# A hybrid DeltaNet and attention trunk on one core: input squares on two engines, first weights behind x, and three small reorderings

## Chip, cores and metric

The kernel runs on one core of one Trainium2 chip. The core has five engines with a queue each: TensorE (PE in the profile) multiplies matrices into PSUM, VectorE (DVE) and ScalarE (ACT) do elementwise work, GpSimd (POOL) sets constants, and SyncE (SP) issues most of the DMAs. Each engine works its queue in order and waits at an instruction until what it needs is there. The metric is the device time of one execution in microseconds (us), lower is better. Given are three runs and one profiled execution.

## The reference

A trunk of two layers over 512 tokens with 1024 channels, in float32. Every mixer and every MLP reads an RMS-normalised copy of the residual stream h and adds its result to h.

```python
def rmsnorm(x, w):
    y = x * lax.rsqrt(jnp.mean(x * x, axis=-1, keepdims=True) + EPS)
    return y * w
...
h = x
# layer 0: gated DeltaNet, then a gated MLP with a causal conv of width 3
h = h + gated_deltanet(rmsnorm(h, a_norm_w), a_w_in, ...)
h = h + conv_gated_mlp(rmsnorm(h, ffn_norm_w[0]), ...)
# layer 1: K and V projected once from h; sliding-window attention, then the MLP
k, v = shared_kv(h, kv_norm_w, w_kv)
h = h + sliding_window_sink_attention(rmsnorm(h, b_norm_w), k, v, b_w_q, ..., b_w_o)
h = h + conv_gated_mlp(rmsnorm(h, ffn_norm_w[1]), ...)
return rmsnorm(h, final_norm_w)
```

Three places of it matter here. The first is the very first norm, with the start of the DeltaNet's input projection (its keys first, then 16 gate pairs per token: a sigmoid, and an exponential of `a_log` times a softplus). The second is the attention's output projection, `o @ w_o`, over 1024 channels of the heads. The third is the end of the last MLP with the final norm.

## The kernel before

**Layout and precision.** The residual stream is held with channels on the 128 partitions and the 512 tokens along the row: eight tiles `hT[0..7]` of 128 x 512. A float32 product is made of three products in a reduced format: each factor is split into a high part and a rest, and `mm3` (L158) sums high x high (L162), high x rest (L163) and rest x high (L164) for each of the eight blocks of 128 channels. A weight block is loaded by SP into a buffer called `stage` (128 x 8 x 256, two buffers), and `cast` (L128) makes the high part `whi` on ScalarE (L132) and the rest `wlo` on VectorE (L133). There are three buffers for each of them.

**What sets the order.** The program is written once, straight through. A planner lays every instruction into its engine's queue: it goes by a priority, which is the program order unless the source says otherwise, and by what it expects to be ready. The source moves priorities for the DeltaNet stage (`ORDER`, L30), fixes TensorE's order by hand in attention (L1357), and can pin one instruction behind another on the same engine with `behind(later, earlier)` (L176), which orders the issue and adds no other wait. Waits on data, on freed buffers and on DMAs are put in by the planner.

**Input stage (L201 to L335).** SP loads the four x tiles of 128 tokens x 1024 channels (L204) and then the first stage of the input projection, the key weights, as two halves of 128 columns (L210). The identity for transposes is made on GpSimd, and five rows of norm weights are loaded on ScalarE's queue and turned into columns, `normc` (L232 to L237). For each x tile `xs[c]`, ScalarE squares it and sums along the row (L258), and takes the root of the mean (L259); VectorE takes the reciprocal (L260) and scales the tile (L261). TensorE then turns each block of 128 channels for all four tiles (L266), and `split_scaled` (L171) makes the high part `xh` on ScalarE (L172) and the rest `xl` on VectorE (L173). Then comes the first key projection, with the conv (L277, L280) and a Silu (L281). The second `stage` buffer is next used for the gates' weights, `gst`: GpSimd clears 48 columns of each block (L307), ScalarE's queue loads two groups of 16 columns (L309, L310), it is cast and multiplied with 48 columns. `nega` takes an Exp of `a_log` (L319); ScalarE's roots and its Exp need different function tables, and a change of table is an instruction of its own in the profile (ACT_TABLE_LOAD). Some further rows, the gates' constants among them, are loaded on SP (L232, L316, L317, L736).

**Output projection of attention (L1320 to L1386).** The eight output tiles need all 16 heads. The first three tiles are opened early, in three PSUM banks `d`, and are filled for the heads that are ready (`early_outputs`, `late_outputs`). The last block of heads comes at L1378 to L1382: nine products, pass by pass (high x high for the three tiles, then rest x high, then high x rest), and an add into `hT[m]` on VectorE after the last of each tile. The loop from L1383 on casts weights for tiles 3 to 7 and multiplies.

**The end (L1100 to L1159).** `final` squares the first seven tiles of the result on ScalarE, sums the squares on VectorE in `acc`, and weights the tiles with the final norm's weights. The last tile's down projection is done in two halves of 256 tokens, each in two parts (`last_down`). When a half is complete, VectorE adds it to `h7` (L1150), and `finish` squares it on ScalarE (L1131), weights it (L1132) and adds the squares to `acc` (L1133) on VectorE; TensorE turns the last four blocks of each of the two token tiles (L1118) and sums `acc` over the channels with a product with a column of ones, one for each token tile (L1137); then come root (L1138) and reciprocal (L1139). Two scaled copies per token tile, one on VectorE (L1146) and one on ScalarE (L1144), go out by SP (L1147). `finish(0)` stands between the two parts of the second half.

Of the kernel before, what the change touches and what calls it, by code (L numbers as in the profile page):

```python
# [17 lines left out]
P = 128  # L18
T = 512
NC = T // P  # L20
D = 1024
# [3 lines left out]
HQK = 8  # L25
# [16 lines left out]
def kernel(  # L42
# [27 lines left out]
    V, S, G, PE, SP = nc.vector, nc.scalar, nc.gpsimd, nc.tensor, nc.sync  # L70
# [130 lines left out]
    xs = []  # L201
# [3 lines left out]
        xs.append(xt)  # L205
    win = a_w_in[0]
    first = wpool.tile([P, 8, 256], F32, tag="stage", bufs=2, name=nm("stage"))
    for i in range(2):
        cs = slice(HQK * P + i * P, HQK * P + (i + 1) * P)
        SP.dma_start(first[:, :, i * P : (i + 1) * P], win[:, cs].rearrange("(k p) c -> p k c", p=P))  # L210
# [44 lines left out]
    for c in range(NC):  # L255
        junk = main.tile([P, D], F32, tag="nt", bufs=2, name=nm("junk"))
        r = const([P, 1], s="rx")
        S.activation(junk[:], xs[c], AF.Square, accum_out=r[:])  # L258
        S.activation(r[:], r[:], AF.Sqrt, bias=epsc[:, 0:1], scale=1.0 / D)  # L259
        V.reciprocal(r[:], r[:])  # L260
        V.tensor_scalar(xs[c][:], xs[c][:], r[:, 0:1], None, op0=ALU.mult)  # L261
    xh, xl = [], []
# [56 lines left out]
    S.activation(nega[32:48, :], gp16[32:48, 0:1], AF.Exp)  # L319
# [780 lines left out]
    def final(h, last_down):  # L1100
        hw, acc = [], None
        for k in range(KD):
            t = r2("xh")
            hw.append(t)
            if k == KD - 1:
                break
            V.tensor_scalar(t[:], h[k], onw_c[:, 9 + k : 10 + k], None, op0=ALU.mult)
            sq = r2("sum" if acc is None else "hsq")
            S.activation(sq[:], h[k], AF.Square)
            if acc is None:  # L1110
                acc = sq
            else:
                V.tensor_tensor(acc[:], acc[:], sq[:], op=ALU.add)

        def turned(hf, c, tag):
            pt = bank(tag)
            for k in range(4):
                PE.transpose(pt[:, k * P : (k + 1) * P], hw[4 * hf + k][:, c * P : (c + 1) * P], ident[:])  # L1118
            return pt

        halves = [bank("d") for _ in range(2)]
        S.activation(warm[:], acc[:, 0:1], AF.Sqrt)
        front = [turned(0, c, t) for c, t in enumerate(["s", "s", "p", "g"])]
        h7, w7 = h[KD - 1], hw[KD - 1]
        sq7 = r2("hsq")
        rt = const([P, NC], s="rt")
        ts = [slice(0, 256), slice(256, 512)]

        def finish(u):
            cs = slice(2 * u, 2 * u + 2)  # L1130
            S.activation(sq7[:, ts[u]], h7[:, ts[u]], AF.Square)  # L1131
            V.tensor_scalar(w7[:, ts[u]], h7[:, ts[u]], onw_c[:, 16:17], None, op0=ALU.mult)  # L1132
            V.tensor_tensor(acc[:, ts[u]], acc[:, ts[u]], sq7[:, ts[u]], op=ALU.add)  # L1133
            back = [turned(1, 2 * u, "d"), turned(1, 2 * u + 1, "s" if u else "d")]
            ps = bank("g")
            for c in (2 * u, 2 * u + 1):
                PE.matmul(ps[:, c : c + 1], acc[:, c * P : (c + 1) * P], onec, start=True, stop=True)  # L1137
            S.activation(rt[:, cs], ps[:, cs], AF.Sqrt, bias=epsc[:, 0:1], scale=1.0 / D)  # L1138
            V.reciprocal(rt[:, cs], rt[:, cs])  # L1139
            for c in (2 * u, 2 * u + 1):  # L1140
                for hf, pt in enumerate((front[c], back[c % 2])):
                    y = r2("xl")
                    if hf:
                        S.activation(y[:], pt[:], AF.Copy, scale=rt[:, c : c + 1])  # L1144
                    else:
                        V.tensor_scalar(y[:], pt[:], rt[:, c : c + 1], None, op0=ALU.mult)  # L1146
                    SP.dma_start(out[0, c * P : (c + 1) * P, hf * T : (hf + 1) * T], y[:])  # L1147

        def add(u):
            V.tensor_tensor(h7[:, ts[u]], h7[:, ts[u]], halves[u][:, 0:256], op=ALU.add)  # L1150
# [12 lines left out]

    def attention(h):
# [192 lines left out]
        with tc.manual_schedule(engines={mybir.EngineType.PE}):  # L1357
            stream = dense()
            for u in range(16):
                scores(u)  # L1360
                if u > 1:
                    values(u - 2)
                if u == 1:
                    take(stream, 8)
                if u > 0:
                    turn_back(u - 1)
                take(stream, 4 if u == 1 else 12 if u < 12 else 11)
            for _ in stream:
                pass
            rest = late_outputs(opened, range(begun, KD - 1))  # L1370
            take(rest, 9)
            turn_back(15)
            values(14)
            take(rest, 5)
            values(15)
            for _ in rest:
                pass
            for i in range(3):  # L1378
                for m, (ps, w) in enumerate(opened):
                    PE.matmul(ps[:], w[i % 2][:, KD - 1, :], (ah, ah, al)[i][-1], start=False, stop=i == 2)  # L1380
# [64 lines left out]
```

## Time and profile before

| what | value |
|---|---|
| median of 3 runs (lowest, highest) | 1416.39 us (1415.27, 1416.59) |
| profiled execution, its own time | 1418.66 us |
| span of the profiled execution | 1416.8 us |
| mean granted TensorE clock | 0.998 |
| busy TensorE, VectorE, ScalarE, GpSimd | 98%, 78%, 53%, 1% |
| first product of the input projection | 13.63 us |
| longest wait of TensorE after that, up to 46 us | 1.72 us |
| start of the last scaled output copy on VectorE | 1411.56 us |
| last output DMA issued | 1413.0 us |

A line of the order of time reads: start, length, engine and source line, operation, output <- inputs by the program's names, shapes, count, and in brackets how long the engine was idle before it and what ended the wait. "SPq" and "ACTq" are DMA issues in a queue, "PEld" is TensorE loading weights, which overlaps its products. Products are pipelined: a product of 512 columns is shown with about 0.39 us, but the next one starts 0.23 us after it. Each of the sums of L1137 is shown as two records.

### The profile page before, as it was taken

The numbers are of one execution on the slowest core, as the hardware profiler recorded it, in microseconds if no ns is written. First come the engines' busy times: TensorE is split into PE (matmuls) and PEld (weight loads), VectorE is DVE, ScalarE is ACT, GpSimd is POOL, SyncE is SP. The second block draws the span as 40 slices with busy tenths as digits, with TensorE's granted clock in tenths as the row PEclk, the third lists the DMA queues.
The fourth block names the chain that finished last, engine by engine and source line by source line (L and its number), as shares of the span: only waits on it lengthen the run. The fifth ranks groups of instructions, "written<-read, shape, count | busy, mean of one in ns | idle before, by whom it ended". The sixth has DMA issues, their size and how long they took to land.

```text
span 1416.8 us, 21740 instructions
## 1 busy us (share of the span) xinstructions
PE 1384.8 (98%) x8362; PEld 1166.5 (82%) x8362; DVE 1109.1 (78%) x2072; ACT 748.0 (53%) x1470; POOL 15.7 (1%) x37
## 2 busy tenths in 40 slices
PE   7999999999999999999999999999999999999997
PEld 5787888878877888888988889778788888988897
DVE  4996886968856447879878889788658888878996
ACT  7764576656647325444335446567544444444543
POOL 1000000000100000000000000000000000000000
PEclk9999999999999999999999999999999999999999
DMA  5333254172465323221443223322132221432222
GB/s 160 90 104 115 80 174 124 60 230 84 143 221 157 119 86 115 90 90 46 134 149 119 75 73 108 109 76 76 60 112 86 93 90 59 137 107 86 95 75 75
DMA packets 162299, 151.80 MB, mean 107 GB/s; under 512 B 24148, under 2 KB 150677, under 8 KB 162197
## 3 DMA queue, kind: packets, MB, share of 16 engines
q1 hardware_dynamic: 159938, 150.22, 33.0%
q8 instruction: 66, 1.08, 0.3%
q10 hardware_dynamic: 2259, 0.20, 0.1%
q14 instruction: 36, 0.29, 0.1%
HBM read 133.60 MB, written 15.75 MB: 105 GB/s over the span
## 4 chain that ended last, share of the span: by engine, by line
PE 85%; DVE 7%; DMA 4%; ACT 2%; issue 1%; SPq 0%; DVEq 0%; ACTq 0%
PE d L162 20%; PE d L164 20%; PE d L163 20%; PE g L198 2%; DVE wlo L133 2%; PE d L1207 1%; PE d L1211 1%; PE d L1209 1%; PE d L1054 1%; PE d L1052 1%; PE d L1053 1%; PE s L1054 1%; PE p L1303 1%; PE s L659 1%; PE s L1052 1%
## 5 line engine op out<-in xcount | busy, mean ns | idle before, releaser
L162 PE MATMUL d<-xh,whi 128*128 128x512 f32 x1128 | 444.2, 394 | 0.2
L163 PE MATMUL d<-xl,whi 128*128 128x512 f32 x1128 | 444.0, 394 | 0.0
L164 PE MATMUL d<-xh,wlo 128*128 128x512 f32 x1128 | 442.1, 393 | 0.8 <-DVE wlo L133 0.5
L132 ACT CAST whi<-stage 128x1024 fp32r<-128x1024 f32 (+2 forms) x234 | 227.4, 976 | 249.7 <-PE d L163 170.3
L133 DVE TENSOR_TENSOR wlo<-stage,whi 128x1024 fp32r<-128x1024 f32 (+2 forms) x234 | 263.3, 1128 | 70.2 <-ACT whi L132 69.3
L164 PEld LDWEIGHTS d<-xh,wlo 128*128 128x128 f32 x1128 | 211.6, 188 | 45.5 <-DVE wlo L133 1.0
L162 PEld LDWEIGHTS d<-xh,whi 128*128 128x128 f32 x1128 | 211.7, 188 | 44.8 <-ACT xh L172 0.5
L163 PEld LDWEIGHTS d<-xl,whi 128*128 128x128 f32 x1128 | 211.7, 188 | 43.1 <-issue 0.5
L280 DVE SCALAR_TENSOR_TENSOR acc<-d,cwc,acc 128x511 f32<-128x511 f32 (+2 forms) x96 | 70.6, 738 | 8.7 <-ACT acc L277 7.8
L913 DVE TENSOR_TENSOR sz<-d,p6s 128x512 f32<-128x512 f32 x59 | 40.6, 688 | 43.4 <-PE d L164 41.2
L935 ACT ACTIVATE dt<-dt 128x512 f32<-128x512 f32 x44 | 27.8, 632 | 78.3 <-DVE dt L918 78.3
L918 DVE SCALAR_TENSOR_TENSOR dt<-sz,fcw,dt 128x511 f32<-128x511 f32 (+1 forms) x60 | 44.8, 747 | 1.8 <-ACT dt L916 0.9
L918 DVE SCALAR_TENSOR_TENSOR va<-sz,fcw,va 128x511 f32<-128x511 f32 (+1 forms) x58 | 43.3, 747 | 0.9
L561 DVE TENSOR_TENSOR sT<-sT,p6s 64x31 f32<-64x31 f32 (+15 forms) x124 | 40.9, 330 | 2.0
L555 DVE TENSOR_TENSOR p6s<-sN,sT 64x31 f32<-64x31 f32 (+15 forms) x124 | 40.7, 328 | 1.9
L1276 ACT ACTIVATE dt<-dt,sm 128x256 f32<-128x256 f32 (+1 forms) x64 | 30.1, 471 | 21.5 <-DVE sm L1259 21.5
L132 ACT CAST whi<-st 128x768 fp32r<-128x768 f32 (+1 forms) x30 | 23.7, 791 | 30.1 <-PE p L1053 5.8
L913 DVE TENSOR_TENSOR zl<-d,p6s 128x512 f32<-128x512 f32 x29 | 20.0, 688 | 17.8 <-PE d L164 17.8
L682 ACT ACTIVATE rq<-o 128x128 f32<-128x128 f32 x64 | 19.0, 301 | 25.0 <-DVE o L677 22.0
L937 DVE TENSOR_TENSOR va<-dt,va 128x512 f32<-128x512 f32 x44 | 30.4, 690 | 1.2
L133 DVE TENSOR_TENSOR wlo<-st,whi 128x768 fp32r<-128x768 f32 (+1 forms) x30 | 26.8, 899 | 2.2 <-ACT whi L132 2.2
L916 ACT ACTIVATE dt<-sz,normc,fcw 128x512 f32<-128x512 f32 x30 | 24.4, 815 | 6.5 <-DVE sz L913 6.2
(769 smaller groups left out, 2873.2 us busy)
## 6 DMA issues: line engine op xcount, KB each, us to landing
stage<-in_ffn_w_up_dram SPq DMA_DIRECT2D x44, 1024.0 KB, 4.7
stage<-in_a_w_in_dram SPq DMA_DIRECT2D x23, 1024.0 KB, 5.5
stage<-in_ffn_w_down_dram SPq DMA_DIRECT2D x16, 768.0 KB, 4.3
stage<-in_a_w_out_dram SPq DMA_DIRECT2D x8, 1024.0 KB, 5.1
st<-in_ffn_w_down_dram SPq DMA_DIRECT2D x8, 768.0 KB, 5.2
zd<-sz SPq DMA_DIRECT2D x16, 256.0 KB, 2.6
od<-o SPq DMA_DIRECT2D x16, 256.0 KB
stage<-in_b_w_q_dram SPq DMA_DIRECT2D x4, 1024.0 KB, 5.0
```

The costliest lines, as they stand in the source:

```text
L132: S.copy(hi[:, :kt, :m], src)
L133: V.tensor_tensor(lo[:, :kt, :m], src, hi[:, :kt, :m].bitcast(F32), op=ALU.subtract)
L162: PE.matmul(ps, hi[:, k, :m], xh[k], start=first and k == 0, stop=False)
L163: PE.matmul(ps, hi[:, k, :m], xl[k][:], start=False, stop=False)
L164: done.append(PE.matmul(ps, lo[:, k, :m], xh[k], start=False, stop=last and k == kt - 1))
L280: V.scalar_tensor_tensor(acc[:, d:], ps[:, : T - d], col, acc[:, d:], op0=ALU.mult, op1=ALU.add)
L555: V.tensor_tensor(tv, N[:, s, s + 1 : 32].unsqueeze(2).to_broadcast([64, n, m]), Tm[:, s : s + 1, 0:m].to_broadcast([64, n, m]), op=ALU.mult,)
L561: V.tensor_tensor(Tm[:, s + 1 : 32, 0:m], Tm[:, s + 1 : 32, 0:m], tv, op=ALU.subtract)
L913: V.tensor_tensor(u[:], ps[:], rs[:], op=ALU.mult)
L918: V.scalar_tensor_tensor(acc[:, d:], u[:, : T - d], tap(2 - d, t), acc[:, d:], op0=ALU.mult, op1=ALU.add)
L937: V.tensor_tensor(b[:], a[:], b[:], op=ALU.mult)
L1276: S.activation(ej, ej, AF.Exp, bias=ngm[:, i : i + 1], scale=-1.0, accum_out=den[:, i : i + 1])
```

## The change

Five edits in three places:

1. The tiles' squares in the input stage alternate: tiles 0 and 2 on ScalarE as before, tiles 1 and 3 on VectorE by a product with an accumulated sum (`tensor_tensor_reduce`).
2. GpSimd copies one column of x tile 2 into each half of the first weight stage before the loads of that stage are issued. The loads overwrite it, so they wait for the copies, and these wait for tile 2.
3. The gates' stage is made and cleared ahead of those copies. The Exp of `a_log` is pinned behind the last root of the input stage.
4. In the output projection of attention, the nine last products go tile by tile, with each tile's add behind its three products.
5. At the end, the add of the last tile's squares on VectorE goes; TensorE sums `acc` and the squares of the last tile by two products into the same column. The weighting is written ahead of the square. The rest of that part of the diff writes the same two halves as a list of cuts and one loop.

```diff
@@ input stage
     first = wpool.tile([P, 8, 256], F32, tag="stage", bufs=2, name=nm("stage"))
+    held_stage = {HQK * P: first}
+    ident = const([P, P], s="ident")
+    make_identity(nc, ident[:])
+    gst = wpool.tile([P, 8, 256], F32, tag="stage", bufs=2, name=nm("gst"))
+    G.memset(gst[:, :, 0:48], 0.0)
+
+    for i in range(2):
+        G.tensor_copy(first[:, 0, i * P : i * P + 1], xs[2][:, 0:1])
     for i in range(2):
         cs = slice(HQK * P + i * P, HQK * P + (i + 1) * P)
         SP.dma_start(first[:, :, i * P : (i + 1) * P], win[:, cs].rearrange("(k p) c -> p k c", p=P))
-    held_stage = {HQK * P: first}
-    ident = const([P, P], s="ident")
-    make_identity(nc, ident[:])
...
     for c in range(NC):
         junk = main.tile([P, D], F32, tag="nt", bufs=2, name=nm("junk"))
         r = const([P, 1], s="rx")
-        S.activation(junk[:], xs[c], AF.Square, accum_out=r[:])
-        S.activation(r[:], r[:], AF.Sqrt, bias=epsc[:, 0:1], scale=1.0 / D)
+        if c % 2 == 0:
+            S.activation(junk[:], xs[c], AF.Square, accum_out=r[:])
+        else:
+            V.tensor_tensor_reduce(
+                out=junk[:], in0=xs[c][:], in1=xs[c][:], scale=1.0, scalar=0.0,
+                op0=ALU.mult, op1=ALU.add, accum_out=r[:],
+            )
+        root = S.activation(r[:], r[:], AF.Sqrt, bias=epsc[:, 0:1], scale=1.0 / D)
...
-    gst = wpool.tile([P, 8, 256], F32, tag="stage", bufs=2, name=nm("gst"))
-    G.memset(gst[:, :, 0:48], 0.0)
...
-    S.activation(nega[32:48, :], gp16[32:48, 0:1], AF.Exp)
+    behind(S.activation(nega[32:48, :], gp16[32:48, 0:1], AF.Exp), root)
@@ final
-        ts = [slice(0, 256), slice(256, 512)]
+        ts = [slice(a * P, b * P) for a, b in CUTS]
         def finish(u):
-            cs = slice(2 * u, 2 * u + 2)
+            c0, c1 = CUTS[u]
+            cs = slice(c0, c1)
+            V.tensor_scalar(w7[:, ts[u]], h7[:, ts[u]], onw_c[:, 16:17], None, op0=ALU.mult)
             S.activation(sq7[:, ts[u]], h7[:, ts[u]], AF.Square)
-            V.tensor_scalar(w7[:, ts[u]], h7[:, ts[u]], onw_c[:, 16:17], None, op0=ALU.mult)
-            V.tensor_tensor(acc[:, ts[u]], acc[:, ts[u]], sq7[:, ts[u]], op=ALU.add)
...
             ps = bank("g")
-            for c in (2 * u, 2 * u + 1):
-                PE.matmul(ps[:, c : c + 1], acc[:, c * P : (c + 1) * P], onec, start=True, stop=True)
+            for c in range(c0, c1):
+                for x in (acc, sq7):
+                    PE.matmul(ps[:, c : c + 1], x[:, c * P : (c + 1) * P], onec, start=x is acc, stop=x is sq7)
...
-        last_down(halves[0][:, 0:256], ts[0], 0)
-        last_down(halves[0][:, 0:256], ts[0], 1)
-        add(0)
-        last_down(halves[1][:, 0:256], ts[1], 0)
-        finish(0)
-        last_down(halves[1][:, 0:256], ts[1], 1)
-        add(1)
-        finish(1)
+        n = len(CUTS)        # CUTS = [(0, 2), (2, 4)]
+        for u in range(n):
+            ps = parts[u][:, 0 : ts[u].stop - ts[u].start]
+            last_down(ps, ts[u], 0)
+            if u > 0:
+                finish(u - 1)
+            last_down(ps, ts[u], 1)
+            V.tensor_tensor(h7[:, ts[u]], h7[:, ts[u]], ps, op=ALU.add)
+        finish(n - 1)
@@ attention
-            for i in range(3):
-                for m, (ps, w) in enumerate(opened):
+            for m, (ps, w) in enumerate(opened):
+                for i in range(3):
                     PE.matmul(ps[:], w[i % 2][:, KD - 1, :], (ah, ah, al)[i][-1], start=False, stop=i == 2)
-                    if i == 2:
-                        V.tensor_tensor(hT[m], hT[m], ps[:], op=ALU.add)
+                V.tensor_tensor(hT[m], hT[m], ps[:], op=ALU.add)
```

More of the change, by code (lines that the diff above doesn't have):

```diff
@@ L257 @@
         r = const([P, 1], s="rx")
-        S.activation(junk[:], xs[c], AF.Square, accum_out=r[:])
-        S.activation(r[:], r[:], AF.Sqrt, bias=epsc[:, 0:1], scale=1.0 / D)
+        if c % 2 == 0:
+            S.activation(junk[:], xs[c], AF.Square, accum_out=r[:])
+        else:
+            V.tensor_tensor_reduce(
+                out=junk[:],
+                in0=xs[c][:],
+                in1=xs[c][:],
+                scale=1.0,
+                scalar=0.0,
+                op0=ALU.mult,
+                op1=ALU.add,
+                accum_out=r[:],
+            )
+        root = S.activation(r[:], r[:], AF.Sqrt, bias=epsc[:, 0:1], scale=1.0 / D)
         V.reciprocal(r[:], r[:])
@@ L1119, in turned @@
             return pt
-        halves = [bank("d") for _ in range(2)]
+        CUTS = [(0, 2), (2, 4)]
+        parts = [bank("d") for _ in CUTS]
         S.activation(warm[:], acc[:, 0:1], AF.Sqrt)
@@ L1126, in final @@
         rt = const([P, NC], s="rt")
[L1127 removed]
+        ts = [slice(a * P, b * P) for a, b in CUTS]
         def finish(u):
[L1130 removed]
+            c0, c1 = CUTS[u]
+            cs = slice(c0, c1)
+            V.tensor_scalar(w7[:, ts[u]], h7[:, ts[u]], onw_c[:, 16:17], None, op0=ALU.mult)
             S.activation(sq7[:, ts[u]], h7[:, ts[u]], AF.Square)
[L1132 to L1134 removed]
+            back = [turned(1, c, "s" if u and c % 2 else "d") for c in range(c0, c1)]
             ps = bank("g")
[L1136 to L1137 removed]
+            for c in range(c0, c1):
+                for x in (acc, sq7):
+                    PE.matmul(ps[:, c : c + 1], x[:, c * P : (c + 1) * P], onec, start=x is acc, stop=x is sq7)
             S.activation(rt[:, cs], ps[:, cs], AF.Sqrt, bias=epsc[:, 0:1], scale=1.0 / D)
             V.reciprocal(rt[:, cs], rt[:, cs])
[L1140 to L1141 removed]
+            for c in range(c0, c1):
+                for hf, pt in enumerate((front[c], back[c - c0])):
                     y = r2("xl")
```

2 lines of the change are left out of this document (removed).

## The prediction

> **What bounds the kernel now.** I read the page first (busy shares and the chain), then the order of time in the three places that the diff touches: the input stage (0 to 46 us), the out-projection of attention (around 1016 us) and the end (from 1403 us).
>
> ```profile
> span 1416.8 us, 21740 instructions
> ...
> PE 1384.8 (98%) x8362; PEld 1166.5 (82%) x8362; DVE 1109.1 (78%) x2072; ACT 748.0 (53%) x1470; POOL 15.7 (1%) x37
> ...
> PE 85%; DVE 7%; DMA 4%; ACT 2%; issue 1%; SPq 0%; DVEq 0%; ACTq 0%
> ```
>
> TensorE (PE) is busy for 98% of the span, and the chain runs through it for 85%. Time can be won only where TensorE waits: before its first product, in short stalls, and after its last product. The diff takes no work from TensorE and adds a few small matmuls at the end.
>
> **The input stage.** Order of time from the start; columns are start, length, engine and line, what it does, and in brackets the idle time before it.
>
> ```profile
> 0.75 2.57 SPq L204 DMA_DIRECT2D xt<-in_x_dram  x4
> ...
> 4.27 1.80 SPq L210 DMA_DIRECT2D stage<-in_a_w_in_dram  x2
> 4.27 1.06 ACT L258 ACTIVATE junk<-xt 128x1024 f32<-128x1024 f32 x1 [1.39 <-DMA xt<-in_x_dram]
> ...
> 5.70 1.06 ACT L258 ACTIVATE junk<-xt 128x1024 f32<-128x1024 f32 x1 [0.28 <-DMA xt<-in_x_dram]
> ...
> 7.07 0.16 DVE L260 RECIPROCAL rx<-rx 128x1 f32<-128x1 f32 x1 [6.05 <-ACT rx L259]
> 7.27 0.75 DVE L261 TENSOR_SCALAR xt<-xt,rx 128x1024 f32<-128x1024 f32 x1
> ...
> 7.94 0.16 DVE L260 RECIPROCAL rx<-rx 128x1 f32<-128x1 f32 x1
> ...
> 8.16 1.06 ACT L258 ACTIVATE junk<-xt 128x1024 f32<-128x1024 f32 x1 [0.94 <-DMA xt<-in_x_dram]
> ...
> 10.54 0.28 DVE L237 COPY normc<-g 128x128 f32<-128x128 f32 x1
> ...
> 11.11 1.03 ACT L132 CAST whi<-stage 128x1024 fp32r<-128x1024 f32 x1
> ...
> 11.44 0.75 DVE L261 TENSOR_SCALAR xt<-xt,rx 128x1024 f32<-128x1024 f32 x1
> ...
> 12.89 0.69 ACT L172 ACTIVATE xh<-s,normc 128x512 fp32r<-128x512 f32 x1 [0.75 <-PE s L266]
> ...
> 13.63 0.80 PE L162 MATMUL d<-xh,whi 128*128 128x512 f32 x1
> ```
>
> All four x tiles are squared, rooted, scaled and turned before the first product (13.63), since a product takes all tokens. The last scaling ends at 11.44 + 0.75 = 12.19. ScalarE (ACT) squares all four; tile 2 arrives at 8.16.
>
> *Squares on two engines.* Tiles 1 and 3 go to VectorE (DVE). What a product with an accumulated sum costs there is not seen in this stage. The nearest rows are attention's score reductions (count, busy us, mean ns of one):
>
> ```profile
> L1259 DVE CUSTOM_DVE_ANT_0 dt<-s,sz,nsink 128x256 f32<-128x256 f32 x30 | 12.9, 480 | 1.6 <-PE s L1251 1.4
> ...
> L1259 DVE CUSTOM_DVE_ANT_0 dt<-s,sz,nsink 128x128 f32<-128x128 f32 x10 | 3.1, 346 | 0.3 <-PE s L1251 0.3
> ```
>
> 128 more columns cost 134 ns, so 1024 cost 480 + 768 x 1.05 = 1284 ns, and with a little for reading the sum out 1.36 us (an estimate from these rows). Now VectorE's whole list: a reciprocal and a scaling take 0.87 us of it per tile (7.07 to 7.94), 3.48 for four; two squares 2.72; the normc copy 0.28. That is 6.48, and it can't begin before tile 1 is there, at 5.70: it ends at 12.18 without a gap, against 12.19 now. So VectorE takes ScalarE's place as this stage's bound and the split wins about nothing: at best 0.3, with the copy after the last scaling. If tile 2's scaling is put ahead of tile 3's square, VectorE waits for tile 2's root and the end slips by about 0.8.
>
> [...]
>
> *First weights held back.* The two loads of L210 now wait for tile 2, by way of two one-column copies on GpSimd (POOL). What moves in the DMA queues when (first 7.0 to 7.5 us, then 8.0 to 8.5 us):
>
> ```profile
> DMA packets 55, 0.21 MB, mean 414 GB/s; under 512 B 1, under 2 KB 5, under 8 KB 55
> ```
>
> ```profile
> DMA packets 294, 0.16 MB, mean 327 GB/s; under 512 B 3, under 2 KB 290, under 8 KB 294
> ```
>
> x moves in packets above 2 KB, these weights in runs of 128 x 4 bytes. At 7 us 50 of 55 packets are still x, at 8 us nearly all are weights: the weights run behind x already, and holding them gives x some tenths at most. It costs them a later start. Tile 2 at about 8.0, two copies and the waits 0.3, then the 3.5 us that the first x tile of the same size took (issued 0.75, used at 4.27): the first half is there at about 11.8, and its cast, now at 11.11, starts 0.7 later. ScalarE's idle 0.75 before 12.89 covers the cast; without that cover it would be paid in full. VectorE's residue of the same weights comes late by as much and may hold up the x residues behind it. On SP the small loads (conv weights, gates' constants, norms) stand behind the held ones, and on GpSimd only memsets stand behind the copies; their users come after 18 us.
>
> *Gates' stage, and the order of the Exp.*
>
> ```profile
> 18.29 1.28 ACT L319 ACT_TABLE_LOAD   x1
> ...
> 19.51 0.55 DVE L133 TENSOR_TENSOR wlo<-gst,whi 128x384 fp32r<-128x384 f32 x1
> ...
> 20.13 3.07 SPq L122 DMA_DIRECT2D stage<-in_a_w_in_dram  x2
> ```
>
> ```profile
> 25.02 0.75 DVE L280 SCALAR_TENSOR_TENSOR acc<-d,cwc,acc 128x509 f32<-128x509 f32 x1
> 25.40 1.05 ACT L132 CAST whi<-stage 128x1024 fp32r<-128x1024 f32 x1 [1.80 <-DMA stage<-in_a_w_in_dram]
> ...
> 45.96 0.48 PE L235 MATMUL g<-ident,f 128*128 128x128 f32 x2 [1.72 <-DVE onwc L237]
> ```
>
> The early clear keeps the memset from standing behind the held copies. If the gates' weights are also cast earlier, their buffer is free before 20.06, the next stage lands before 25.40, and ScalarE's run of activations can start when the conv sum is there (25.77) instead of after that cast (26.45): up to 0.7 off TensorE's one long stall here, the 1.72 before 45.96. The Exp's table load is pinned behind the last root; it falls into ScalarE's idle time (no gain: TensorE didn't wait for it) or ahead of the weights' cast. I count both at nothing, bounds -0.7 and +1.3 (one table load).
>
> Input stage together: +0.4, taken between the two orders on VectorE; bounds -0.9 and +1.6, as not all ends meet. Behind it TensorE runs almost without a gap, so it passes to the end.
>
> **The out-projection's last products.** Nine products (three open tiles, last k) go tile by tile instead of pass by pass.
>
> ```profile
> 1014.75 0.69 DVE L169 TENSOR_TENSOR at<-p,at 128x512 fp32r<-128x512 f32 x1 [6.44 <-ACT at L168]
> ...
> 1015.06 0.85 PE L1380 MATMUL d<-at,whi 128*128 128x512 f32 x3
> ...
> 1016.44 0.84 PE L1380 MATMUL d<-at,whi 128*128 128x512 f32 x3
> 1016.87 2.95 ACT L132 CAST whi<-stage 128x1024 fp32r<-128x1024 f32 x3 [2.14 <-PE d L1380]
> ...
> 1017.97 0.50 PE L162 MATMUL d<-sy,whi 128*128 128x512 f32 x1 [0.68 <-ACT whi L132]
> ...
> 1018.67 3.49 DVE L133 TENSOR_TENSOR wlo<-stage,whi 128x1024 fp32r<-128x1024 f32 x3
> ```
>
> The open tiles hold all three buffers of high weights. The next tile's cast (1016.87) waits for the seventh product, the first tile's last. In the new order that is the third. Products start 0.23 apart (1015.06 to 1016.44 for six), so it ends 4 x 0.23 = 0.92 earlier, and the three casts, which pace TensorE's next products, move with it. The third product needs the low half of the last heads, ready at 1014.75 + 0.69 = 1015.44, and would start at 1015.52: just in time. Late next is the cast itself, about 1 us per tile, so the later part of the stall stays. -0.9, bounds -0.95 and -0.5 (if VectorE's residues, behind three adds, become late). What follows hangs on TensorE, so it is kept.
>
> **The end.** The chain that ended last, and the last turn of a block from the order of time:
>
> ```profile
> 1406.12 0.35 PE g L1137 x4
> ...
> 1406.99 1.41 DVE xl L1146 x2
> 1408.40 0.34 DVE pz L1150
> ...
> 1408.76 0.43 ACT acc L1131
> ...
> 1409.21 0.44 DVE ol L1133
> ...
> 1409.78 0.59 PE g L1137 x4
> ```
>
> ```profile
> 1409.34 0.27 PE L1118 MATMUL s<-ident,xh 128*128 128x128 f32 x1
> ```
>
> Removed: the add L1133, 0.44 on the chain. Added: a second matmul for each of four columns, 2 records each (now 4 records for two columns). In the first half 4 more records lie on the chain, 0.35 by the row and at most 0.45; they delay the roots, the two scalings L1146, and the add L1150 that stands behind these on VectorE. In the second half the squares are ready at 1409.19, but TensorE turns two blocks until 1409.61 and then has 8 records instead of 4. It can start on them about 0.4 earlier than now and needs 0.4 more: they end where they end now. So +0.4 and 0: TensorE's own work covered the step that goes. Bounds -0.4 (if the first half's records are hidden) and +0.5. The weighting that now comes ahead of the square is on another engine: nothing.
>
> **Sum.** +0.4 - 0.9 + 0.4 = -0.1. The profiled execution took 1418.66 (1.86 around its span), 2.27 above the median of 1416.39. It becomes 1418.6, and the median 1416.3. 0.2% (2.8 us) is about what a measurement of this kernel can tell from no change.
>
> **Rivals.**
>
> *The early chain moves* (faster). A planner sets the order of issue from what is ready; with other starts it may close the whole stall of 1.72 at 45.96, and the end's records may be hidden. For it: ScalarE and VectorE set that stall, and ScalarE sits idle for 1.80 before 25.40. Against: VectorE is full up to 12.2. It gives -1.7 - 0.9 + 0 = -2.6, 1413.8; a little more would be told from no change. Chance 0.22.
>
> *VectorE squares at half rate* (slower). By the rows a square is 212 ns fixed and 1.05 a column; at half rate it takes 2.36 instead of 1.28. Two of them on the engine that is full: +2.2, and the sum is 0.4 + 2.2 - 0.9 + 0.4 = +2.1, 1418.5. It decides from the first square on. Against it, a form with two f32 sources in SBUF takes 746 ns for 511 columns here, 1.05 a column if the fixed part is the same:
>
> ```profile
> L918 DVE SCALAR_TENSOR_TENSOR dt<-sz,fcw,dt x60: 733/746/753, 535.0 to 1348.6; 128x511 f32<-128x511 f32 x30, 128x510 f32<-128x510 f32 x30
> ```
>
> But it has no accumulator. Chance 0.1. [...]
>
> *The held weights come too late* (slower). If small loads or the Exp get ahead of them, their cast starts after 11.9, and from there each microsecond is one at the first product. Held loads start about 4 us later than now; if 2 us more than the cover arrives, the sum is +1.9, 1418.3. Chance 0.16.
>
> **Chances.** Forecast 0.52 (-1.3 to +1.1), the rivals 0.22, 0.1 and 0.16. The range, 1413.8 to 1418.4, reaches to the prices of the rivals and leaves out less than 2 in 10. Faster by over 0.2%: the upper part of the first rival and its meeting with other good ends, 0.17. Slower by over 0.2%: where the slower cases meet, 0.12. Within: 0.71.
>
> **What would show it.** Right: two reductions of about 1.3 us on VectorE and the first product at 13.6 to 14.4; the cast behind L1380 about 0.9 earlier against its products, and no stall ahead of the fourth tile; 8 records of the sums in each half, with the last add still behind L1146. Wrong: the first product before 13.2 or after 15; no stall around 45 us; a shorter way from the last product to the end.

## The result, and the profile after

The changed kernel takes 1426.48 us (median of 4 runs, 1424.1 to 1428.82) against 1416.49 (4 runs, 1415.27 to 1418.15): ratio 1.0067, 95% interval 1.0054 to 1.008. The forecast was 1416.3 and its range ended at 1418.4; the kernel is 10 us slower. The profiled execution took 1428.82, its span is 10.2 longer than that of before, and the mean granted clock fell from 0.998 to 0.994. The page:

```profile
span 1427.0 us, 21757 instructions
...
PE 1392.1 (98%) x8370; PEld 1171.0 (82%) x8370; DVE 1111.3 (78%) x2074; ACT 747.6 (52%) x1467; POOL 14.9 (1%) x39
...
PEclk9999999999989999999999999999999999999999
...
PE 87%; DVE 6%; DMA 2%; ACT 2%; issue 1%; DVEq 0%; ACTq 0%
```

TensorE's busy time grew by 7.3 us, though the change gives it only eight more records of 0.25 us at most: most of the loss is products that take longer, not waiting. The one slice with an 8 in the clock's row is the 12th of 40, around 420 us, in a stage that the change doesn't touch.

**The front.** Order of time after; the lines of before that they answer to stand in the prediction.

```profile
5.97 1.23 DVE L267 CUSTOM_DVE_ANT_0 junk<-xt 128x1024 f32<-128x1024 f32 x1 [4.95 <-DMA xt<-in_x_dram]
...
7.31 0.76 DVE L279 TENSOR_SCALAR xt<-xt,rx 128x1024 f32<-128x1024 f32 x1
...
8.08 0.30 POOL L217 COPY stage<-xt 128x1 f32<-128x1 f32 x2 [6.45 <-DMA xt<-in_x_dram]
8.17 3.47 DVE L279 TENSOR_SCALAR xt<-xt,rx 128x1024 f32<-128x1024 f32 x1
...
8.31 0.52 POOL L338 MEMSET sz<- 80x512 f32 x1
...
8.49 1.02 SPq L220 DMA_DIRECT2D stage<-in_a_w_in_dram  x2
...
9.29 1.80 POOL L410 MEMSET Xg<- 128x2048 f32 x1
...
11.63 1.20 DVE L267 CUSTOM_DVE_ANT_0 junk<-xt 128x1024 f32<-128x1024 f32 x1
...
13.18 1.28 ACT L335 ACT_TABLE_LOAD   x1
...
14.81 1.04 ACT L132 CAST whi<-stage 128x1024 fp32r<-128x1024 f32 x1
15.76 0.68 ACT L172 ACTIVATE xh<-s,normc 128x512 fp32r<-128x512 f32 x1
...
16.49 0.79 PE L162 MATMUL d<-xh,whi 128*128 128x512 f32 x1 [0.76 <-ACT xh L172]
```

The squares cost VectorE 1.23 and 1.20, as expected. But a scaling of 0.76 takes 3.47 the second time: it runs while GpSimd clears sz, gr, sk and Xg, which the held copies have pushed from the first microseconds to 8.31. The root of tile 3, the table load, the cast and the first product follow one by one, and the first product comes at 16.49 instead of 13.63.

**Further on.** TensorE's wait at 46 us has become longer, and another one than before (1.72 for `onwc`):

```profile
43.83 0.40 PE L163 MATMUL d<-xl,whi 128*128 128x512 f32 x1
46.98 0.50 PE L164 MATMUL d<-xh,wlo 128*128 128x512 f32 x1 [2.75 <-DVE wlo L133]
```

Then the windows (length, busy us and count of TensorE, its weight loads, VectorE, ScalarE, GpSimd, then the granted clock, the busy share of the DMA engines and their GB/s), after and before:

```profile
48.15:51.56 3.41, 3.41 (x10) 2.60 (x9) 2.50 (x3) 0.14 (x1) 0.00 (x0) 0.50 0.69 193
...
416.79:427.03 10.24, 9.13 (x96) 7.33 (x96) 6.49 (x10) 4.49 (x9) 0.30 (x1) 0.50 0.52 164
```

```profile
48.15:51.56 3.41, 3.41 (x21) 2.75 (x20) 2.94 (x6) 2.89 (x5) 0.00 (x0) 1.00 1.01 316
...
416.79:427.03 10.24, 7.02 (x42) 6.04 (x43) 4.97 (x13) 5.88 (x21) 0.00 (x0) 1.00 0.82 272
```

For 3.41 us and for 10.24 us TensorE has half its clock, which costs up to 1.7 and 5.1. Before has no such gap between 16 and 1412 us. What TensorE does just ahead of the long one is the last pass of DeltaNet's triangular solver, a run of small products of 32 and 64 rows (L585 to L612 before, L601 to L628 after). Its products before, from 402.7 to 409 us (count, busy us, mean ns, and idle time):

```profile
L612 PE MATMUL s<-sy,p6s 64*64 64x64 f32 x32 | 1.8, 226 | 0.0
L164 PE MATMUL d<-xh,wlo 128*128 128x512 f32 x4 | 1.7, 423 | 0.0
L162 PE MATMUL d<-xh,whi 128*128 128x512 f32 x3 | 1.4, 464 | 0.0
L163 PE MATMUL d<-xl,whi 128*128 128x512 f32 x3 | 1.2, 393 | 0.0
L585 PE MATMUL s<-Xg,nt 32*32 32x32 f32 x16 | 0.9, 194 | 0.0
```

and after, from 414.6 to 422.8:

```profile
L628 PE MATMUL s<-sy,p6s 64*64 64x64 f32 x32 | 2.6, 274 | 1.0 <-ACT p6s L624 1.0
...
L621 PE MATMUL p<-Xg,nt 64*64 64x64 f32 x16 | 1.1, 318 | 0.5 <-DVE Xg L612 0.5
L608 PE MATMUL s<-pz,sy 32*32 32x32 f32 x16 | 1.1, 237 | 0.8 <-ACT pz L604 0.8
...
L162 PE MATMUL d<-kT,whi 128*128 128x512 f32 x1 | 0.8, 793 | 0.0
```

Before, ten products of 512 columns stand between the small ones, and TensorE never waits. After, there is one, at the pass's end; TensorE waits for ScalarE and VectorE inside the pass, and the clock drops. The large products have been used up earlier: the planner has made another order of issue. Against before's, some 360 of TensorE's rows stand elsewhere, nearly all of them ahead of 460 us, in the DeltaNet stage.

**The two other parts.** Out-projection and end, after:

```profile
1026.15 0.39 PE L1396 MATMUL d<-at,whi 128*128 128x512 f32 x1
...
1027.13 2.94 ACT L132 CAST whi<-stage 128x1024 fp32r<-128x1024 f32 x3 [1.31 <-PE d L1396]
...
1028.32 0.41 PE L162 MATMUL d<-sy,whi 128*128 128x512 f32 x1
...
1028.43 1.22 DVE L133 TENSOR_TENSOR wlo<-stage,whi 128x1024 fp32r<-128x1024 f32 x1
```

```profile
1417.37 1.41 DVE L1164 TENSOR_SCALAR xl<-s,rt 128x512 f32<-128x512 f32 x2
...
1418.70 0.41 DVE L1174 TENSOR_TENSOR pz<-pz,d 128x256 f32<-128x256 f32 x1
```

The cast comes 0.98 behind the first of the nine products instead of 1.81, and the residue 2.28 instead of 3.61. The last add still stands behind the first half's scalings.

How much later each product starts than the same product before (medians over 25 us of before's time; the columns on the right are experiments that follow):

| us of before | after | 8: split alone | 14: pinned, eighth | 13: pinned, fifth | 9: tiles 0, 2 | 10: no split | 3: out-proj. alone |
|---|---|---|---|---|---|---|---|
| start of the first product (before 13.63) | 16.49 | 15.73 | 13.81 | 14.31 | 13.24 | 18.69 | 14.00 |
| 25 to 50 | +3.9 | +3.5 | -0.2 | +0.6 | -0.9 | +2.8 | 0.0 |
| 75 to 100 | +6.6 | +6.6 | +2.3 | +0.6 | +0.5 | +4.4 | +0.2 |
| 375 to 400 | +7.8 | +7.9 | +5.2 | +3.9 | +0.6 | +5.6 | +0.1 |
| 475 to 500 | +11.1 | +11.1 | +8.0 | +3.8 | -0.9 | +3.7 | -1.2 |
| 975 to 1000 | +11.1 | +10.0 | +7.0 | +3.6 | -1.9 | +3.1 | -2.4 |
| 1050 to 1075 | +9.9 | +10.1 | +7.0 | +3.6 | -1.9 | +1.9 | -3.6 |
| 1375 to 1400 | +9.9 | +10.0 | +7.1 | +3.6 | -0.9 | +2.2 | -3.5 |

One profile is one run: the waits of 2.0 at 428 us and 0.9 at 720 in before's profile are missing in several others, and the profile of 13 has a gap of 3.41 us in its clock at 303 us. Steps under 2 us in this table mean little unless they repeat. The step between 975 and 1050 does: -1.2 to -1.3 in every kernel that has the out-projection's change, and 0 in those that don't.

### The profile page after: what moved, and what is told of

Its sections match the earlier page's. It is cut to its first block, busy times and chain, and to the rows that moved or that the text cites. A ratio compares the mean times of both kernels' runs of the same rounds, so it can differ in the third digit from the quotient of the medians.

```text
span 1427.0 us, 21757 instructions
## 1 busy us (share of the span) xinstructions
PE 1392.1 (98%) x8370; PEld 1171.0 (82%) x8370; DVE 1111.3 (78%) x2074; ACT 747.6 (52%) x1467; POOL 14.9 (1%) x39
## 4 chain that ended last, share of the span: by engine, by line
PE 87%; DVE 6%; DMA 2%; ACT 2%; issue 1%; DVEq 0%; ACTq 0%
PE d L164 20%; PE d L162 20%; PE d L163 19%; PE g L198 2%; PE d L1070 1%; DVE wlo L133 1%; PE d L1223 1%; PE d L1227 1%; PE d L1225 1%; PE d L1068 1%; PE d L1069 1%; PE s L1070 1%; PE s L667 1%; PE s L1068 1%; PE s L1069 1%; PE s L675 1%
```

## The experiments

The theory after reading the two traces (Theory 1): the copies that hold the weights push GpSimd's memsets under VectorE's scaling (the collision), and the rest is a consequence of the late start. Rival 2: the cost is the order of issue that the planner makes of the changed front. Rival 4: the held weights come too late. A third rival, squares at half rate, fell with the 1.23 above. Each ratio is against the kernel before on the same chip, with its 95% interval.

**1. Memsets first.** In the changed kernel, moved up from their old places (sk with its selects too):

```diff
+    R = row("sz")
+    G.memset(R[0:80, :], 0.0)
+    gr = row("gr", F32R)[:, :]
+    G.memset(gr.bitcast(F32), 0.0)
...
+    Xg = main.tile([P, 4, T], F32, tag="Xg", bufs=1, name="Xg")
+    G.memset(Xg[:], 0.0)
     for i in range(2):
         G.tensor_copy(first[:, 0, i * P : i * P + 1], xs[2][:, 0:1])
```

> The changed kernel with one thing moved: the memsets and selects on GpSimd (rows sz and gr, sk, Xg) are issued ahead of the two copies that wait for the input, everything else as changed. Theory 1 (GpSimd's memsets, pushed behind the input's arrival, block VectorE's scaling): the scaling of 3.47 falls to about 0.76, the first product comes at 13.6 to 14.2 instead of 16.49, the clock gaps at 45 and 416 us go, and the time is 1414 to 1417. Rival 2 (the planner's other order, which the split of the squares brings, costs most of it later): the front gains its 2.7, the offset behind 45 us stays, 1421 to 1424. Rival 4 (the held weights are late): the scaling shortens, and the first product stays at 16 or later behind the cast of the weights.

1.002 (1.001 to 1.0031), 1421.7 against 1417.7. No scaling is blocked, and the gap at 416 us is gone. But the first product comes at 19.02: with other starts the planner has put the held loads behind the small ones on SP (at 11.14) and the cast of the weights behind six input rows (at 17.93). So it has Rival 4's front, and less than half of the loss. The edit had also changed the order of issue: TensorE's differs from before's in some 50 rows, no longer in some 360. It couldn't tell Theory 1 from Rival 2.

**2. The collision alone**, in the kernel before:

```diff
+    late = const([P, 1], s="late")
+    G.tensor_copy(late[:], xs[2][:, 0:1])
```

> The kernel before, with the gates' stage cleared early and one small copy on GpSimd that waits for the third input tile, ahead of the memsets of gr, sk and Xg; no split of squares, no held weights, old out-projection and end. The copy's result is used by nobody. Theory 1: one of VectorE's scalings between 8 and 13 us takes 2.5 to 3.5 instead of 0.75, and the first product comes 1 to 3 us later than 13.63; if the later loss of 7 us follows from a late start alone, 1420 to 1427; if it doesn't, 1417 to 1420. Rival 2 (order): the scaling may be blocked, the time stays within 2 us of 1416.5 as the order of issue hardly differs from before. A rival by which the memsets only happen to run then: no scaling over 1.0.

1.0146 (1.0127 to 1.0164), 1439.79: 22 us slower, which no theory allowed. The scaling took 1.67, which explains 1. The rest is in the products of 512 columns, which start further apart all along the kernel at a granted clock of 1.00 (109 records instead of 112 in the 25 us from 475, 775 and 1075); experiments 5 and 12 find what it came with.

**3 and 4. The out-projection alone, and the end alone**, each as in the change's diff.

> The kernel before with the out-projection's last products taken tile by tile, nothing else. The prediction's step: -0.9 (bounds -0.95 to -0.5), 1415.6. The offsets of the two traces give -1.3, 1415.2. A rival by which the -1.3 came from the clock or the later start: no change, 1416.5. In the profile: the cast of the attention's first operand about 0.9 earlier against the products.

> The kernel before with the end's change alone: the squares of the last tile summed by TensorE, no add on VectorE, the weighting ahead of the square. The prediction's step: +0.4 (bounds -0.4 to +0.5), 1416.9. The two traces' offsets give +0.2 to +0.3. A rival by which the add's removal pays: -0.4, 1416.1. In the profile: four records per pair of columns, the last add of a tile behind the first half's scalings.

Out-projection: 0.9988 (0.9976 to 1.0), 1416.04 against 1417.7; -1.24 at its place in the trace. End: 0.9997 (0.9986 to 1.0007), not to be told from no change; in its trace the stretch from the last product that both kernels share to the end of the span is 0.28 longer.

**5. The collision without the new tile.** As 2, but the copy goes into a column of the gates' stage that nobody reads, so that no tile is added, and no row in the order of issue changes on TensorE, VectorE, ScalarE or SP:

```diff
+    G.tensor_copy(gst[:, 0, 255:256], xs[2][:, 0:1])
```

> The kernel before, gates' stage cleared early, one GpSimd copy that waits for the third input tile ahead of the memsets of sz, gr, sk and Xg; the copy goes into a column of the gates' stage that nobody reads, so no tile is added and no tile moves in SBUF; the order of issue of all other engines is that of before. Theory 1 (memsets behind the copy block VectorE): one scaling takes 1.5 to 3.5 instead of 0.75, the first product comes by as much later, and the time is 1417.5 to 1420 against 1417.7 on this chip before. The rival that the collision alone costs 22 us, as the run with the scratch tile could be read: 1435 or more. The rival that the scratch tile's 4 bytes made every product longer: a 512-column product is back at 223 ns apart, and the time is within 3 of before.

```profile
8.30 0.50 POOL L218 COPY gst<-xt 128x1 f32<-128x1 f32 x1 [6.21 <-DMA xt<-in_x_dram]
...
10.04 1.55 DVE L264 TENSOR_SCALAR xt<-xt,rx 128x1024 f32<-128x1024 f32 x1
...
14.61 0.80 PE L162 MATMUL d<-xh,whi 128*128 128x512 f32 x1
```

1.0011 (1.0002 to 1.002): the collision is real, 0.8 on the scaling and 1.0 on the first product, and costs about 1.5 us (0.3 to 2.8) when the order stays. That is no 10.

**6 and 7. The change without the two copies, and with the copies on ScalarE.**

```diff
-        G.tensor_copy(first[:, 0, i * P : i * P + 1], xs[2][:, 0:1])
```

```diff
-        G.tensor_copy(first[:, 0, i * P : i * P + 1], xs[2][:, 0:1])
+        S.copy(first[:, 0, i * P : i * P + 1], xs[2][:, 0:1])
```

> The changed kernel without the two GpSimd copies: the first weights are sent at once and GpSimd's memsets run in the first microseconds, and all else, the order of issue too, is as changed (a few rows differ). Theory 1 (the hold, by its collision and by late weights, costs it all): scaling 0.75, first product at 13.0 to 14.2, no clock gaps at 48 and 416, 1414 to 1418. Rival 2 (the other order of issue): the front is mended, a clock gap at 416 and the other offsets stay, 1420 to 1424.

> The changed kernel with the two copies that hold the weights made by ScalarE, not GpSimd: the weights are held as before, GpSimd has nothing to wait for and its memsets run early; order of issue otherwise as changed. Theory 1 in its narrow form (the collision on VectorE is the cost, not the hold): scaling 0.75, first product at 13.5 to 14.5, 1415 to 1418. Rival 4 (held weights late, cast behind them and the Exp): first product at 15 or later, 1419 to 1424. Rival 2: front mended, 1420 to 1424 by a gap in the clock later.

1.0065 (1.0053 to 1.0077) and 1.0059 (1.0047 to 1.0071). GpSimd's memsets run in the first microseconds, every scaling takes 0.75, and the kernel is as slow as with the collision. Theory 1 falls. TensorE's order of issue differs from the change's in 3 and 2 rows, and the gap of the clock is there: 6.83 us long at 417, 10.24 at 415. That is Rival 2's side, but its 1420 to 1424 was too low for both (1426.56 and 1426.3).

**8. The split alone**, tiles 1 and 3 on VectorE, in the kernel before, with nothing held and no other edit.

> The kernel before with the squares on two engines, nothing else; its order of issue is the changed kernel's, not that of before. Theory 1: nothing to collide with, first product within 0.6 of before's 13.63, 1415 to 1419. Rival 2 (the order of issue that comes with the split costs several us): 1420 to 1424, with a gap in the clock at 416 or a new stall ahead of it.

1.0081 (1.0066 to 1.0097), 1428.54: the split of the squares alone gives the whole loss, more than the 1420 to 1424 expected of Rival 2. The first view is the long gap in the clock, the second ScalarE's order of time at the front:

```profile
417.21:427.45 10.24, 9.19 (x96) 7.32 (x96) 6.49 (x10) 4.52 (x8) 0.30 (x1) 0.50 0.58 176
```

```profile
11.27 1.04 ACT L132 CAST whi<-stage 128x1024 fp32r<-128x1024 f32 x1
12.21 0.20 ACT L365 CAST skr<-sk 128x16 fp32r<-128x16 f32 x1
13.64 0.51 ACT L132 CAST whi<-gst 128x384 fp32r<-128x384 f32 x1 [1.23 <-DMA f<-in_final_norm_w_dram]
14.05 1.04 ACT L132 CAST whi<-stage 128x1024 fp32r<-128x1024 f32 x1
15.00 0.68 ACT L172 ACTIVATE xh<-s,normc 128x512 fp32r<-128x512 f32 x1
```

Freed from tile 3's square, ScalarE gets three casts that nobody needs yet ahead of the first input row, one of which waits 1.23 for a transfer: the first product comes at 15.73. And the order differs from before's in 360 rows further on.

**9. The other two tiles.** The same split with tiles 0 and 2 on VectorE:

```diff
-        if c % 2 == 0:
+        if c % 2 == 1:
             S.activation(junk[:], xs[c], AF.Square, accum_out=r[:])
```

> The kernel before with the squares of the input's tiles 0 and 2 on VectorE and 1 and 3 on ScalarE, nothing else: as many squares on each engine as in the change, the other way round. With this the planner keeps the order of before from the first weights on (one row of TensorE's differs; with tiles 1 and 3 it was 360). Rival 2 (the order that the planner makes of the split is the cost, not the split): 1415 to 1418.5, no gap in the clock at 416, first product at 13.0 to 14.2. If the split itself costs (VectorE busier, ScalarE's casts out of step): 1424 or more, as with tiles 1 and 3.

```profile
10.72 1.03 ACT L132 CAST whi<-stage 128x1024 fp32r<-128x1024 f32 x1
12.50 0.69 ACT L172 ACTIVATE xh<-s,normc 128x512 fp32r<-128x512 f32 x1 [0.75 <-PE s L278]
...
13.24 0.80 PE L162 MATMUL d<-xh,whi 128*128 128x512 f32 x1
```

1.0009 (1.0 to 1.0019). The same work on each engine, one row of TensorE's order changed instead of 360, and some 10 us less. Here ScalarE squares the last tile; that this leaves the planner no free time there to fill with casts is the likely reason, and wasn't tried.

**10. The change without the split**: all squares on ScalarE, the rest as changed.

> The changed kernel with all four squares back on ScalarE; the held weights, the early clearing, the pinned Exp, the out-projection and the end as changed. The planner's order is near that of before again. Rival 2: it loses the clock gap at 416 and 1416 to 1420 is left: -1.4 of the out-projection, +1 to +3 of a late first product (collision and held weights). Theory 1 as it stood: 1424 to 1427, since the copies and the memsets behind them are still there.

1.0023 (1.0012 to 1.0033), 1421.14, a little above the 1416 to 1420 expected. The collision is there in full (a scaling of 3.19), the first product comes at 18.69 behind the late weights, and still two thirds of the loss are gone, with the gap at 416. Held weights and collision cost some 4 us in this order (3.3 and the 1.2 that the out-projection gives back, less the end's 0.3).

**11. Tiles 0 and 2 with the out-projection's change.**

> The kernel before with the squares of tiles 0 and 2 on VectorE and the out-projection's last products tile by tile: the parts of the change that should pay, in the order of before. By the rows of the out-projection -1.2 to -1.6, and by the split -0.5 to +0.5: 1415 to 1416.5 where before is 1417.7. The rival, that even a small change at the front brings a gap in the clock: 1419 or more.

0.9996 (0.9985 to 1.0007), 1416.8 against 1417.16, just above the expected range. The split brings nothing even in the good order. The out-projection alone (experiment 3) stays the best version, and its gain is at the edge of what can be told.

**12. An unused tile of 4 bytes**, in the kernel before:

```diff
+    late = const([P, 1], s="late")
+    G.memset(late[:], 0.0)
```

> The kernel before with one more tile of 4 bytes a partition, cleared by GpSimd at the start and read by nobody: no copy that waits, no collision. If the 22 us of the earlier run came from the tile's moving all later tiles by its size in SBUF, the 512-column products stand 233 to 234 ns apart again instead of 227 and the time is 1436 to 1441. If they came from the collision with that run's order: 1416 to 1420, and 227 ns.

1.013 (1.0116 to 1.0145), 1435.46, 18 us slower. Two windows of the feed-forward part, before and with the tile:

```profile
750.00:775.00 25.00, 25.00 (x112) 20.70 (x111) 21.45 (x32) 12.34 (x17) 0.00 (x0) 1.00 0.28 94
```

```profile
750.00:775.00 25.00, 25.00 (x109) 20.07 (x108) 18.78 (x28) 11.52 (x16) 0.00 (x0) 1.00 0.26 84
```

TensorE is busy throughout at the full clock in both, and does 109 records in the time of 112. That answers experiment 2: most of its 22 us came with the added tile, not with the collision. The change itself is not of this kind: its products of 512 columns start 227 ns apart, as before's do, and 233 in experiments 2 and 12 (an estimate: 227 x 112 / 109, by the records from 775 to 800).

**13 and 14. The same split, two pins.** The kernel of experiment 8, and every cast of weights after the first is pinned in order of issue behind one of the eight input rows, the fifth in 13 (below) and the eighth, `xh_made[7]`, in 14:

```diff
-        S.copy(hi[:, :kt, :m], src)
+        made = S.copy(hi[:, :kt, :m], src)
+        if pins:
+            behind(made, pins[0])
...
     key_proj(0, 0)
+    pins.append(xh_made[4])
```

> The kernel before with the squares split as in the change (tiles 1 and 3 on VectorE), and the casts of all later weights pinned in order of issue behind the fifth of the eight input rows that ScalarE writes. With this pin the planner gives back the order of before on TensorE (3 rows differ). If the order is the cause and not which tiles are where: 1415.5 to 1419, no gap in the clock at 416. If tiles 1 and 3 on VectorE cost by themselves: 1424 or more.

> The same, pinned behind the eighth input row. The casts no longer stand ahead of the input rows, but from there on the planner keeps the order of the split alone (5 rows of TensorE's differ from that). If the front's order is the cause of it all: 1416 to 1420. If the order further on costs by itself (a longer wait at 46 us, the triangular solver's small products without large ones around them and the clock's gap at 416): first product at 13.2 to 14.2, the gap stays, 1422 to 1427.

13: 1.0008 (0.9994 to 1.0021). 14: 1.0058 (1.0042 to 1.0073). In 14 the front is whole, as the order of time shows, and what follows is not:

```profile
13.07 0.69 ACT L176 ACTIVATE xh<-s,normc 128x512 fp32r<-128x512 f32 x1 [0.93 <-PE s L283]
...
13.81 0.80 PE L166 MATMUL d<-xh,whi 128*128 128x512 f32 x1
```

```profile
42.77 0.80 PE L168 MATMUL d<-xh,wlo 128*128 128x512 f32 x1 [2.74 <-DVE wlo L137]
```

```profile
412.00:416.00 4.00, 2.63 (x104) 2.28 (x104) 1.72 (x5) 2.58 (x5) 0.00 (x0) 0.84 0.59 176
414.73:424.97 10.24, 9.19 (x72) 7.29 (x63) 6.49 (x10) 4.58 (x9) 0.30 (x1) 0.50 0.58 181
```

The split is the same, the first product is within 0.2 of before's, and the wait of 2.74, the uncovered pass and the gap are all there, for some 8 us. In 13 the planner gives back the order of before (3 rows differ), and the last pass of the solver has its cover:

```profile
406.60:412.90 6.30, 6.30 (x139) 4.69 (x137) 2.63 (x6) 2.19 (x5) 0.30 (x1) 1.00 0.65 210
```

So about 8 of the split's 10 to 11 us (6 to 10 by the interval of 14) come from the order further on, and the 2 to 3 that remain from the casts ahead of the input rows. The long gap at 416 is in all five profiles with the change's order (the change, 6, 7, 8, 14) and in none of the nine with before's layout and its order, or nearly (before, 1, 3, 4, 5, 9, 10, 11, 13). The executions without a trace agree: the mean granted clock that each reports has medians of 0.9935 to 0.995 in the five kernels and of 0.997 or more in the nine. The short gap of 3.41 us between 45 and 52 us is another matter: it stands in 5, 9, 10 and 11 too, with before's order or nearly, and so isn't the new order's.

## Why the prediction was wrong, point by point

**The step that failed** is the one that closes the input stage: "Behind it TensorE runs almost without a gap, so it passes to the end." The stage's own term was too small as well (+0.4, at most +1.6, and the first product came 2.86 later), but that is not most of the 10 us. The sum took the change at the first product and carried it on unchanged. It left out that the order of issue of the next 450 us is made from the same starts. Experiments 8, 9, 13 and 14 show this: equal work at the front, and 1.0081, 1.0009, 1.0008 and 1.0058 by the order alone. The planner did stand in the prediction, in the first rival, but only with a gain: "with other starts it may close the whole stall of 1.72 at 45.96". In its place stands a wait of 2.75. No price was put on the case that it makes a worse order.

**The squares on VectorE.** 1.36 estimated with the sum's read-out, 1.23 and 0.08 measured. That "the split wins about nothing" held as far as the engines' own times go: 1.0009 in the good order. The rival with half the rate, 2.36 for a square, fell with the first row. No run shows that rate or the +2.2 that the rival put on it: the change's two squares took 1.23 and 1.20, and those of the eight experiments with squares on VectorE (1, 6, 7, 8, 9, 11, 13, 14) 1.20 to 1.23.

**"on GpSimd only memsets stand behind the copies; their users come after 18 us."** True of the users, wrong as a price. The memsets themselves held up VectorE: 0.76 became 3.47 in the change, 0.75 became 1.55 in experiment 5, which prices it at about 1.5 us in before's order. In the change's own order taking it away wins nothing that can be measured (1.0065 without the copies against 1.0067), as casts then take its place ahead of the first input row. In the change's trace it goes the other way too: a select on GpSimd took 1.13 (at 11.76) while VectorE squared, instead of 0.20 before. Why the two engines hold each other up, no trace shows. Before's trace had a hint that wasn't read: a scaling of 16 columns on VectorE took 0.88 under a memset on GpSimd at 20.15, and 0.26 in the trace after.

**The held weights.** By the prediction "the first half is there at about 11.8" and is cast 0.7 late: the cast came at 14.81 in the change and at 17.93 in experiment 1. In the change it didn't wait for the weights at the end: sent at 8.49 and with 4.0 us from issue to landing, they would be there near 12.5 (an estimate from these two numbers of the trace), and the cast stood in ScalarE's queue behind the late root, the table load and the Exp. The rival "The held weights come too late" named the Exp and the small loads, and was right about what happens at the front. Its +1.9 was too small for its own case (about 4 us with the collision, experiment 10) and it isn't what makes the 10 us.

**The table load** was counted at nothing, with up to +1.3. It lies between tile 3's root and the cast, on the way to the first product. How much of its 1.28 is paid was not tried.

**The out-projection**: -0.9, bounds -0.95 to -0.5. Measured: -1.24. The cast gained 0.83. The term was too small because "the later part of the stall stays" was wrong: with two adds instead of three ahead of it, VectorE's residue of the next weights came 1.33 earlier.

**The end**: +0.4, bounds -0.4 to +0.5; measured +0.28 in the traces, in experiment 4 and in the change alike. Eight records a half and the last add behind the scalings, as said.

**The sum** then reads: the split +10 to +11, nearly all by the order of issue; out-projection -1.2; end +0.3; hold and collision nothing that experiments 6 and 7 could measure in this order. That makes 9 to 10, and the measured difference is 10.0. Single terms are known to some 2 us, so the agreement is partly luck.

Why the clock drops at 416 is not shown. The gaps are 3.41, 6.83 and 10.24 us long, one, two and three times the shortest, at a granted clock of 0.50. Ahead of the long one in the change, TensorE was busy for 2.16 of 3.41 us (413.38 to 416.79), all of it products of 32 and 64 rows. Before was busy for only 1.71 of the 3.41 us from 422.54 on, in products of 128 rows, and kept its clock at 1.00. By these two stretches the busy share alone doesn't decide it. That products with few rows count for less there is a guess of the author's that fits both. No run here put other work into the pass to test it.

## What to carry to other kernels

Where a planner makes the order of issue, an edit at the start has two prices: that of the engines' times, and that of the new order. Compare the two orders before summing anything, and give the second a price of either sign; if the order moves far beyond the edit, choose the variant of the edit that keeps it (the other two tiles, or a pin on the casts). And ask of each operation that moves not only who needs it, but which engine runs beside it in its new place.

## What was not expected of the hardware

- One unused tile of 4 bytes a partition made the whole kernel 1.3% slower in experiment 12 (1.0116 to 1.0145). In the feed-forward stage the 512-column products start 227 ns apart before; from 775 to 800 us TensorE does 112 records before, and 109 with this tile and with the scratch tile of experiment 2, at the same granted clock of 1.00. What about the tile does it wasn't tried. The kernel's own unused tiles ("gap" in their names) stand in this light.
- In the change's trace memsets on GpSimd, which read nothing, held up a VectorE scaling with one input: 0.76 became 3.47 beside 2.8 us of memsets in a row (8.31 to 11.09).
- At the start the profile prints a granted clock of 1.00, though its record of the clock only begins at 16.35 us before and 20.85 after. The lengths of the products tell more: 0.80 for the first ones, 0.39 soon after the record begins. From the first product to the start of the record it is 2.72 before and 4.36 after; if the clock is half until then, the difference costs another 0.8 (an estimate from these rows).
